# Modulation products of a two-layer mixer network: units of 256 columns behind every second block, in place of 128 columns behind each

## The chip, the cores and the metric

The kernel runs on one core of a Trainium2 chip. The metric is the device time of one execution in microseconds, the median of a few runs. Besides these runs, one execution was taken by the hardware profiler; everything said below of single instructions comes from that one.

## What is computed

The reference is a network of two layers over 512 latent and 256 context tokens of 1024 features. Each layer first turns the conditioning vector `c` (for the latent tokens) and `c_ctx` (for the context tokens) into six vectors of 1024 numbers, the modulation: shift, scale and gate of the first half of the layer, shift, scale and gate of the second.

```python
m_lat = jnp.split((silu_c @ ada_w[l] + ada_b[l])[:, None, :], 6, axis=-1)
m_ctx = jnp.split((silu_cc @ ada_w[l] + ada_b[l])[None, None, :], 6, axis=-1)
xn_lat = modulate(rmsnorm(h_lat, norm1_w[l]), m_lat[0], m_lat[1])
...
h_lat = h_lat + m_lat[2] * merge_branches(...)
h_lat = h_lat + m_lat[5] * conv_ffn(modulate(rmsnorm(h_lat, norm2_w[l]), m_lat[3], m_lat[4]), ...)
```

`ada_w[l]` is 1024 by 6144. The product has two rows only (one for each conditioning vector), but it reads all 25 MB of the matrix in each layer. The rest of a layer is an input projection, three mixers (an mLSTM, an attention with shared keys, a gated delta net), their merge and output projection, and a gated feed forward network with a short convolution.

## The kernel before, in words

**Large products.** `gemm_fm` (L227) makes a product feature-major, one block of 128 output columns at a time. For a block it loads raw weights (`wraw`, L208, one DMA from SyncE's queue into one of 3 slots of 4 KB in each partition, tag `wraw`), splits them into a high and a low float32r part (`wsplit`, L216: a copy on ScalarE, a subtraction on VectorE), multiplies (`mm3`, L241: three matmuls for each of 8 blocks of the contraction, high by high L248, high by low L249, low by high L250, first for the 512 latent tokens, then for the 256 context tokens where they count), and hands the PSUM banks to `done`, which evicts them.

**The modulation in between.** The first 16 of the 96 blocks of 128 modulation columns are made at the start of the kernel, 512 columns at a time (`ada_mm`, L428). The other 80 are made one by one in `ada_unit` (L457), called at three kinds of place: after each block of `gemm_fm` while the counter `self.nada` is above zero (L235 to L239), and four in a row in `ada_fill` (L473) three times, where the norm of the next part is being made. The counter is set to 32 in the mixers of layer 0, to 16 in the feed forward part of layer 0 and to 20 in the mixers of layer 1.

A unit works like this. Its raw weights, 8 blocks of 128 rows by 128 columns (512 KB), come through the same `wraw` slots. Then the transpose of the unit before is issued (`ada_fin`, L481). Then come 8 float32 matmuls (L467): the stationary operand is 32 columns wide, of which two count, and four blocks of the contraction lie side by side in the four column groups of the array. The profile shows two records for each of these matmuls, 16 for a unit. ScalarE copies the result out of PSUM (L470). In the next call of `ada_fin` the TensorE turns it (L489) and VectorE adds the four groups (L491); with every eighth block of columns the bias is added.

```python
def ada_unit(self):
    ...
    raw = self.wraw(self.I["ada_w"][l][:, 128 * g:128 * g + 128], KD, 128, f"ad{l}_{g}")
    self.ada_fin()
    ps = self.adps[0](f"adp{l}_{g}")
    for k in range(KD):
        j = k % 4
        nc.tensor.matmul(ps[32 * j:32 * j + 32, 0:128], self.s32[:, 2 * k:2 * k + 32], raw[:, k, :],
                         start=(k < 4), stop=(k >= 4), tile_position=(0, 32 * j))
    rw = self.T([128, 128], f"adr{l}_{g}", tag="adr")
    nc.scalar.copy(rw, ps[:, 0:128])
```

**PSUM.** The unit's product takes a bank of tag `pc` in the mixers and in the feed forward part. There is one such bank, and in the mixers of layer 0 it is also the one that the context tokens of the large products use. The transpose takes one of the two banks `pl` of the latent tokens in the mixers, and a bank `pa` in the feed forward part.

**What sets the order.** The program is traced in the order of `PLAN` (L43), and a scheduler that simulates the engines then puts the instructions of each engine in order: of those that are ready it takes the one with the highest priority. The scans of the delta net (`g0`, `g1`) and the attention (`ga`) have high priorities, the large products and the units fill the time in between. So a unit or a block of a product can be cut: small steps of a scan are put between its matmuls. SyncE's queue issues nearly all DMAs, strictly in its own order.

Of the kernel before, what the change touches and what calls it, by code (L numbers as in the profile page):

```python
# [16 lines left out]
D = 1024  # L17
# [12 lines left out]
# columns of the input projection  # L30
# [5 lines left out]
# token tiles 0..3 are latent, 4 and 5 context; scan orders of the two directions  # L36
ORDER = ((4, 5, 0, 1, 2, 3), (5, 4, 3, 2, 1, 0))

# The mixers of each layer: the order in which their parts are traced, the priorities of the parts and of the weights
# (the long chains of small steps first, the large products in between), the PSUM of the context tokens in P1.  # L40
# P0, P1: projections of the delta net's pairs of heads, g0, g1: their scans; qp, ga: attention; mp, ml: mLSTM;
# cz, ao, mg: gates; n: from here on columns of the modulation in between.
# [51 lines left out]
class Kernel:  # L94
# [7 lines left out]
    # ---------------------------------------------------------------- pools  # L102
# [18 lines left out]
    # slots of the mixers' phase: a.. for the delta net, b.. for the others, gs for the projections  # L121
# [21 lines left out]
    # slots of the phase of the merge and the feed forward  # L143
# [12 lines left out]
    # PSUM banks: latent and context tokens of the large products, the delta net, the others  # L156
# [3 lines left out]
    def p0(self):  # L160
        """Banks of the latent tokens: those of the context tokens too where there are none."""
        self.turn = not self.turn
        return self.pb if self.spare and self.turn else self.pl
# [14 lines left out]
    # ---------------------------------------------------------------- small helpers  # L178
    def rsqrt(self, out, z, n, nm, who="n"):
        """out = z ** -0.5 for [128, n] float32 z (bit trick and Newton steps)."""  # L180
# [19 lines left out]
    def split(self, h, l, x, eng=None):  # L200
        """x = h + l, both in float32r."""
# [5 lines left out]
    # ---------------------------------------------------------------- weights  # L207
    def wraw(self, src, nk, ncols, nm, slot=None):  # L208
        """raw weights [128, nk, ncols] from src rows (k p), columns given."""
        t = slot(nm) if slot else self.T([128, 1024], nm, tag="wraw", bufs=3)  # L210
# [16 lines left out]
    def gemm_fm(self, src, c0, ncols, nk, segs, done, nm):  # L227
        """Feature-major product: columns c0.. of src [nk*128, *] as stationary, tokens moving.
        segs: list of (token range, xh [128, nk, n], xl), latent first.
        done(block, [(psum, token range)]) takes the result."""  # L230
        for b in range(ncols // 128):
# [3 lines left out]
            if self.nada:  # L235
                self.nada -= 1
                self.ada_unit()
                if self.nada == 0:
                    self.ada_fin()  # L239
# [14 lines left out]
    def first_weights(self, src, c0, nk, nm, slot=None):  # L254
        """Weights for gemm_first."""
# [16 lines left out]
    def first_part(self, segs, nk, k0, k1, a, e):  # L272
        """Blocks k0.. of the contraction for the tokens a..."""
# [4 lines left out]
        for k in range(k0, k1):  # L278
            for b in range(2):
                ps = self.fp[s][b][:, sl]  # L280
                hw, lw = self.fw(k, b)
                # one accumulation group for the bank
# [4 lines left out]
    def gemm_first(self, nk, segs, done, nm, begun=False):  # L287
        """gemm_fm of two blocks, side by side, that can start with the first block of features."""
# [8 lines left out]
    def gemm_tail(self, src, segs, done, nm, slot, nxt=None):  # L297
        """Feature-major product over two blocks of the contraction, all of its D columns, by groups of 256 tokens;
        done(block, token range, psum)."""
# [18 lines left out]
    def gemm_tm(self, src, c0, ncols, xs, done, nm, nlat=0):  # L318
        """Token-major product in groups of 256 columns: done(group, [(pair of tiles, psum)]); the first nlat groups
        for the latent tokens only."""  # L320
        nc = self.nc
        for g in range(ncols // 256):
            pss = [(self.pl if i < 2 else self.pc)(f"{nm}p{g}_{i}") for i in range(2 if g < nlat else 3)]
            for half in range(2):
# [3 lines left out]
                for i, ps in enumerate(pss):  # L328
                    for u in range(2):
# [3 lines left out]
                        for kk in range(4):  # L333
                            k = 4 * half + kk
                            xh, xl = xs[s][1][:, k, o:o + 128], xs[s][2][:, k, o:o + 128]
                            # one accumulation group for the bank
# [5 lines left out]
    # ---------------------------------------------------------------- setup  # L342
# [360 lines left out]
    def gates(self, l, xs):  # L703
# [102 lines left out]
        def c4(d, tt):                                              # columns of (dir, tile) in 48s  # L806
            return slice(24 * d + 4 * tt, 24 * d + 4 * tt + 4)
# [1106 lines left out]
```

## Time and profile before

| | |
|---|---|
| median of 3 runs | 2726.53 us (2725.04 to 2727.49) |
| span of the profiled execution, first to last instruction | 2715.6 us |
| TensorE busy | 2663.0 us, 98% |
| TensorE weight loads busy | 2261.6 us, 83% |
| VectorE, ScalarE, GpSimd busy | 58%, 37%, 9% |
| mean granted TensorE clock | 0.994 |
| modulation matmuls (L467), busy | 65.5 us |

The profiler gives no whole-execution time beside the span; the median of the runs lies 10.9 us above the span. Below, PE is the TensorE's matmul stream, PEld its weight loads (which overlap it), DVE is VectorE, ACT ScalarE, POOL GpSimd, SP SyncE, and L with a number is a line of the kernel. A TensorE record lasts from the entry of its first column until its results are out, so records of successive matmuls overlap; the cost of a matmul in a stream is the distance from its start to the next start.

### The profile page before, as it was taken

Reading aid. Unit: us, or ns where it says so; the run is one execution under the profiler, and the core shown is the slowest. Engines: PE = TensorE matmul, PEld = TensorE weight load, DVE = VectorE, ACT = ScalarE, POOL = GpSimd, SP = SyncE. Lnnn points to the kernel's source line nnn. Section 1 sums busy time; section 2 is a strip of 40 time slices with the busy share of each in tenths; the row PEclk is TensorE's granted clock in tenths of the full one; section 3 lists DMA queues with packets and bytes.
Section 4 is the critical chain, followed back from the end, with each engine's and each line's share of the span. In section 5 each row is a group of like instructions: output and inputs, shape, how many; then the busy total and the mean of one; then the engine's idle time right before and its main releaser. Section 6 shows DMA issues by size and latency. Waiting matters only on the chain.

```text
span 2715.6 us, 46016 instructions
## 1 busy us (share of the span) xinstructions
PE 2663.0 (98%) x18041; PEld 2261.6 (83%) x18041; DVE 1573.4 (58%) x3527; ACT 998.5 (37%) x2269; POOL 235.0 (9%) x234
## 2 busy tenths in 40 slices
PE   7999999999999999999999999999999999999999
PEld 5887988788888888888888899888877777888887
DVE  6775665756524655444444577867675646655555
ACT  5433354333322234232232254444633332433332
POOL 1000000000000410010010120000000003100000
PEclk9999999999999999999999999999998999999999
DMA  8354332556746423412212254422376675333332
GB/s 281 96 162 127 90 113 80 155 149 172 210 145 223 140 88 104 140 47 74 66 47 78 61 152 121 138 61 79 114 215 179 169 237 156 114 95 95 93 97 86
DMA packets 523466, 342.97 MB, mean 126 GB/s; under 512 B 48007, under 2 KB 488561, under 8 KB 522481
## 3 DMA queue, kind: packets, MB, share of 16 engines
q1 hardware_dynamic: 522961, 336.88, 42.2%
q8 instruction: 142, 2.33, 0.3%
q10 hardware_dynamic: 288, 3.15, 0.3%
q14 instruction: 75, 0.61, 0.1%
HBM read 283.92 MB, written 56.03 MB: 125 GB/s over the span
## 4 chain that ended last, share of the span: by engine, by line
PE 88%; DMA 5%; DVE 3%; ACT 1%; issue 1%; SPq 1%; POOL 0%; DVEq 0%; ACTq 0%; POOLq 0%
PE mg04p L249 2%; PE mg04p L250 2%; PE adp L467 2%; PE mg04p L248 2%; PE y0p L248 1%; PE y0p L250 1%; PE y0p L249 1%; PE mg14p L248 1%; PE mg14p L250 1%; PE mg14p L249 1%; PE y1p L248 1%; PE y0op L248 1%; PE y0op L250 1%; PE y0op L249 1%; PE y1p L249 1%
## 5 line engine op out<-in xcount | busy, mean ns | idle before, releaser
L1714 POOL TENSOR_TENSOR f0a<-f0a,f0g 128x768 f32<-128x768 f32 x22 | 40.7, 1848 | 486.8 <-DVE f0a L1702 486.8
L467 PE MATMUL adp<-ad,s 128*32 128x128 f32 x1280 | 65.5, 283 | 2.7 <-DVE cz0t L903 2.4
L1714 POOL TENSOR_TENSOR f1a<-f1a,f1g 128x512 f32<-128x512 f32 x22 | 28.5, 1294 | 315.4 <-DVE f1a L1702 284.4
L467 PEld LDWEIGHTS adp<-ad,s 128*32 128x32 f32 x1280 | 33.9, 110 | 26.0 <-issue 9.9
L1716 DVE TENSOR_TENSOR f0gl<-f0a,f0gh 128x768 fp32r<-128x768 f32 x22 | 21.1, 959 | 58.4 <-ACT f0gh L1715 58.4
L1715 ACT CAST f0gh<-f0a 128x768 fp32r<-128x768 f32 x22 | 18.3, 832 | 76.6 <-POOL f0a L1714 76.6
L1638 POOL TENSOR_TENSOR y0a<-y0a,y0g 128x768 f32<-128x768 f32 x16 | 33.0, 2062 | 129.9 <-DVE y0g L1635 127.6
L470 ACT COPY adr<-adp 128x128 f32<-128x128 f32 x80 | 21.2, 265 | 39.7 <-PE adp L467 39.3
L901 ACT ACTIVATE mg0t<-mg04p 128x512 f32<-128x512 f32 (+1 forms) x40 | 19.4, 486 | 38.5 <-PE mg04p L250 28.2
L1708 ACT ACTIVATE f0g<-f0g 128x768 f32<-128x768 f32 x22 | 18.5, 845 | 33.2 <-DVE f0g L1702 33.2
L1638 POOL TENSOR_TENSOR y1a<-y1a,y1g 128x512 f32<-128x512 f32 x16 | 23.9, 1494 | 78.3 <-DVE y1g L1635 78.3
L491 DVE TENSOR_REDUCE ada<-adc 128x2 f32<-128x8 f32 x80 | 12.9, 161 | 27.9 <-PE adc L489 27.6
L1635 DVE SCALAR_TENSOR_TENSOR y0g<-y0g,y0p 128x512 f32<-128x512 f32 (+1 forms) x32 | 17.4, 549 | 15.7 <-PE y0p L250 14.7
L1708 ACT ACTIVATE f1g<-f1g 128x512 f32<-128x512 f32 x22 | 13.8, 631 | 32.9 <-DVE f1g L1702 32.9
L979 DVE SCALAR_TENSOR_TENSOR m0mb<-m0mb,g0a,cst 128x128 f32<-128x128 f32 x48 | 14.0, 346 | 18.4 <-DMA m0mb<-g0rd 18.4
L489 PE MATMUL adc<-cst,adr 128*128 128x128 f32 x80 | 22.2, 278 | 0.4 <-ACT adr L470 0.4
L1659 DVE SCALAR_TENSOR_TENSOR hr<-y0op,y0gh,hr 128x512 f32<-128x512 f32 (+1 forms) x16 | 9.8, 615 | 21.0 <-PE y0op L250 21.0
L1002 PE MATMUL m0n<-m0vb,m0mb 128*128 128x129 f32 x96 | 19.1, 299 | 1.1 <-issue 1.1
L1611 DVE TENSOR_TENSOR y0l<-y0ld,y0h 128x768 fp32r<-128x768 f32 x12 | 13.0, 1093 | 12.2 <-ACT y0h L1610 12.2
L1734 DVE SCALAR_TENSOR_TENSOR hr<-f0d8p,ada,hr 128x512 f32<-128x512 f32 (+1 forms) x16 | 9.9, 618 | 15.7 <-PE f0d8p L250 15.7
L1734 DVE SCALAR_TENSOR_TENSOR hr<-f0d12p,ada,hr 128x512 f32<-128x512 f32 (+1 forms) x16 | 9.9, 618 | 15.7 <-PE f0d12p L250 15.7
L1734 DVE SCALAR_TENSOR_TENSOR hr<-f0d4p,ada,hr 128x512 f32<-128x512 f32 (+1 forms) x16 | 9.9, 618 | 15.7 <-PE f0d4p L250 15.7
(3922 smaller groups left out, 9921.5 us busy)
## 6 DMA issues: line engine op xcount, KB each, us to landing
ad<-ada_w SPq DMA_DIRECT2D x96, 512.0 KB, 4.0
mg04r<-w_in SPq DMA_DIRECT2D x20, 512.0 KB, 5.2
mg14r<-w_in SPq DMA_DIRECT2D x20, 512.0 KB, 5.1
y0g<-mg SPq DMA_DIRECT2D x24, 384.0 KB, 4.2
mg<-mg0t SPq DMA_DIRECT2D x24, 256.0 KB, 2.0
y0r<-w_branch SPq DMA_DIRECT2D x12, 512.0 KB, 3.9
mg<-mg1t SPq DMA_DIRECT2D x24, 256.0 KB, 4.3
y1r<-w_branch SPq DMA_DIRECT2D x12, 512.0 KB, 4.2
```

The costliest lines, as they stand in the source:

```text
L248: nc.tensor.matmul(o, hv[:, k, :], xh[:, k, :], start=(k == 0), stop=False)
L249: nc.tensor.matmul(o, hv[:, k, :], xl[:, k, :], start=False, stop=False)
L250: nc.tensor.matmul(o, lv[:, k, :], xh[:, k, :], start=False, stop=(k == nk - 1))
L467: nc.tensor.matmul(ps[32 * j:32 * j + 32, 0:128], self.s32[:, 2 * k:2 * k + 32], raw[:, k, :], start=(k < 4), stop=(k >= 4), tile_position ...
L470: nc.scalar.copy(rw, ps[:, 0:128])
L489: nc.tensor.transpose(ps[:, 128:256], rw, self.ident)
L901: nc.scalar.activation(s, o, AF.Tanh, scale=0.5)
L1638: nc.gpsimd.tensor_tensor(out=a[:, :nt], in0=a[:, :nt], in1=gt[:, :nt], op=ALU.add)
L1708: nc.scalar.activation(a[:, :nt], a[:, :nt], AF.Silu)
L1714: nc.gpsimd.tensor_tensor(out=a[:, :nt], in0=a[:, :nt], in1=keep[b][:, :nt], op=ALU.mult)
L1716: nc.vector.tensor_tensor(out=gl[:, k, :nt], in0=a[:, :nt], in1=gh[:, k, :nt].bitcast(F32), op=ALU.subtract)
L1734: nc.vector.scalar_tensor_tensor(out=hv[:, a:b], in0=ps, scalar=self.ada[l][:, 40 + j, (a >= SEQ):(a >= SEQ) + 1], in1=hv[:, a:b], op0=ALU ...
```

## The change

Units of 256 columns take the place of units of 128: 40 units where there were 80. Each loads its weights with two DMAs of 4 blocks by 256 columns (512 KB each, in two `wraw` slots), issues 8 matmuls of 256 columns and one copy of 256 columns; `ada_fin` turns it with two transposes and reduces it with one instruction. A new function `ada_next` takes the place of the lines in `gemm_fm`: it counts the blocks as before, but calls `ada_unit` at every second one only, the first among them. `ada_fill` is called for 2 units instead of 4. The raw weights have 4 slots instead of 3 (also where the gates' weights are loaded, L674), and the scratch for dynamic DMA is set to 1024. The other lines of the diff remove comments.

```diff
 def wraw(self, src, nk, ncols, nm, slot=None):
-        t = slot(nm) if slot else self.T([128, 1024], nm, tag="wraw", bufs=3)
+        t = slot(nm) if slot else self.T([128, 1024], nm, tag="wraw", bufs=4)
...
 def gemm_fm(self, src, c0, ncols, nk, segs, done, nm):
...
             done(b, self.mm3(hv, lv, nk, segs, f"{nm}p{b}"))
-            if self.nada:
-                self.nada -= 1
-                self.ada_unit()
-                if self.nada == 0:
-                    self.ada_fin()
+            self.ada_next()
...
 def ada_unit(self):
-        raw = self.wraw(self.I["ada_w"][l][:, 128 * g:128 * g + 128], KD, 128, f"ad{l}_{g}")
+        W = self.I["ada_w"][l]
+        raws = [self.wraw(W[512 * q:512 * q + 512, 256 * g:256 * g + 256], 4, 256, f"ad{l}_{g}_{q}") for q in range(2)]
         self.ada_fin()
         ps = self.adps[0](f"adp{l}_{g}")
-        for k in range(KD):
-            j = k % 4
-            nc.tensor.matmul(ps[32 * j:32 * j + 32, 0:128], self.s32[:, 2 * k:2 * k + 32], raw[:, k, :],
-                             start=(k < 4), stop=(k >= 4), tile_position=(0, 32 * j))
-        rw = self.T([128, 128], f"adr{l}_{g}", tag="adr")
-        nc.scalar.copy(rw, ps[:, 0:128])
+        for q, raw in enumerate(raws):
+            for j in range(4):
+                k = 4 * q + j
+                nc.tensor.matmul(ps[32 * j:32 * j + 32, 0:256], self.s32[:, 2 * k:2 * k + 32], raw[:, j, :],
+                                 start=(q == 0), stop=(q == 1), tile_position=(0, 32 * j))
+        rw = self.T([128, 256], f"adr{l}_{g}", tag="adr")
+        nc.scalar.copy(rw, ps[:, 0:256])
...
+def ada_next(self):
+        if self.nada:
+            self.nada -= 1
+            if self.nada % 2:
+                self.ada_unit()
+            if self.nada == 0:
+                self.ada_fin()
...
 def ada_fin(self):
-        nc.tensor.transpose(ps[:, 128:256], rw, self.ident)
-        a = self.ada[l][:, g:g + 1, :]
-        nc.vector.tensor_reduce(out=a, in_=ps[:, 128:256].rearrange("p (o j r) -> p o r j", o=1, j=4)[:, :, 0:2, :],
+        for b in range(2):
+            nc.tensor.transpose(ps[:, 256 + 128 * b:384 + 128 * b], rw[:, 128 * b:128 * b + 128], self.ident)
+        nc.vector.tensor_reduce(out=self.ada[l][:, 2 * g:2 * g + 2, :],
+                                in_=ps[:, 256:512].rearrange("p (o j r) -> p o r j", o=2, j=4)[:, :, 0:2, :],
                                 axis=AX.X, op=ALU.add)
...
-                    self.ada_fill(4)
+                    self.ada_fill(2)
...
-    nc = bacc.Bacc("TRN2", target_bir_lowering=False, num_devices=1)
+    nc = bacc.Bacc("TRN2", target_bir_lowering=False, num_devices=1,
+                   dynamic_dma_scratch_size=1024)
```

## Rows read from the trace of the kernel before

**Rows 1.** The page: span, busy time of each engine, clock in 40 slices.
```profile
span 2715.6 us, 46016 instructions
...
PE 2663.0 (98%) x18041; PEld 2261.6 (83%) x18041; DVE 1573.4 (58%) x3527; ACT 998.5 (37%) x2269; POOL 235.0 (9%) x234
...
PEclk9999999999999999999999999999998999999999
```

**Rows 2.** The page: share of the chain that ended last, by engine.
```profile
PE 88%; DMA 5%; DVE 3%; ACT 1%; issue 1%; SPq 1%; POOL 0%; DVEq 0%; ACTq 0%; POOLq 0%
```

**Rows 3.** The page's costliest groups: busy us, mean ns of one, idle before, releaser.
```profile
L467 PE MATMUL adp<-ad,s 128*32 128x128 f32 x1280 | 65.5, 283 | 2.7 <-DVE cz0t L903 2.4
...
L470 ACT COPY adr<-adp 128x128 f32<-128x128 f32 x80 | 21.2, 265 | 39.7 <-PE adp L467 39.3
...
L489 PE MATMUL adc<-cst,adr 128*128 128x128 f32 x80 | 22.2, 278 | 0.4 <-ACT adr L470 0.4
```

**Rows 4.** Timeline of PE around one unit, feed forward, layer 0: start, duration, instructions.
```profile
1057.71 0.28 PE L250 MATMUL f0g02p<-n01xh,f0g02s0l 128*128 128x256 f32 x1
1057.83 0.27 PE L489 MATMUL adc<-cst,adr 128*128 128x128 f32 x1
1058.03 0.64 PE L467 MATMUL adp<-ad,s 128*32 128x128 f32 x16
1058.61 0.49 PE L248 MATMUL f0g02p<-n01xh,f0g02s1h 128*128 128x512 f32 x1
```

**Rows 5.** Groups of PE's lines: the records of the 512-column units, columns as in rows 3.
```profile
L438 PE MATMUL ad<-ad,s 128*32 128x512 f32 x64 | 10.1, 599 | 2.0 <-issue 1.2 <-DMA ad<-ada_w 0.8
```

**Rows 6.** Timeline of PE at the start: two units of 512 columns, three transposes.
```profile
41.09 3.64 PE L438 MATMUL ad<-ad,s 128*32 128x512 f32 x32
44.66 0.55 PE L449 MATMUL adc<-cst,adr 128*128 128x128 f32 x3
```

**Rows 7.** Timeline of PE: the first unit that is cut, and the last piece of all.
```profile
228.54 0.40 PE L250 MATMUL aq0p<-n00xh,aq0s1l 128*128 128x512 f32 x1
228.86 0.64 PE L467 MATMUL adp<-ad,s 128*32 128x128 f32 x14
229.43 0.24 PE L1545 MATMUL c00z<-c00XT,c00N 32*32 32x32 f32 x2
229.60 0.41 PE L467 MATMUL adp<-ad,s 128*32 128x128 f32 x2
229.94 0.43 PE L1220 MATMUL b0a4po<-b0a4P,b0v 128*64 128x128 f32 x2
...
2339.18 0.41 PE L467 MATMUL adp<-ad,s 128*32 128x128 f32 x2
```

**Rows 8.** Waits of PE: who waited for whom, us in total, times, longest.
```profile
PE adp L467 <- DVE cz0t L903: 2.4, 1, 2.4
...
PE g1ps L691 <- DVE g1w L205: 1.1, 1, 1.1
...
PE mg14p L248 <- ACT mg1t L901: 1.1, 1, 1.1
...
PE g0ps L691 <- DVE g0w L205: 1.0, 1, 1.0
...
PE bp0p L337 <- ACT bp0s_0h L204: 0.8, 1, 0.8
...
PE mg04p L248 <- ACT mg0t L901: 0.7, 1, 0.7
```

**Rows 9.** Waits of SyncE's queue: the longest in total.
```profile
SPq L213 <- PE adp L467: 238.4, 57, 26.3
```

**Rows 10.** DMA issues: the modulation's weights, KB each, median us to landing.
```profile
ad<-ada_w SPq DMA_DIRECT2D x96, 512.0 KB, 4.0
```

**Rows 11.** Windows: busy time, then granted clock, DMA share, GB/s.
```profile
1005.00:1155.00 150.00, 147.70 (x1133) 125.90 (x1132) 79.47 (x158) 52.46 (x100) 9.63 (x8) 1.00 0.41 120
...
2062.00:2076.00 14.00, 13.79 (x76) 10.08 (x78) 4.82 (x20) 4.04 (x9) 0.00 (x0) 0.52 0.39 115
```

More of the change, by code (lines that the diff above doesn't have):

```diff
@@ L488, in ada_fin @@
         ps = self.adps[1](f"adc{l}_{g}")
-        nc.tensor.transpose(ps[:, 128:256], rw, self.ident)
-        a = self.ada[l][:, g:g + 1, :]
-        nc.vector.tensor_reduce(out=a, in_=ps[:, 128:256].rearrange("p (o j r) -> p o r j", o=1, j=4)[:, :, 0:2, :],
+        for b in range(2):
+            nc.tensor.transpose(ps[:, 256 + 128 * b:384 + 128 * b], rw[:, 128 * b:128 * b + 128], self.ident)
+        nc.vector.tensor_reduce(out=self.ada[l][:, 2 * g:2 * g + 2, :],
+                                in_=ps[:, 256:512].rearrange("p (o j r) -> p o r j", o=2, j=4)[:, :, 0:2, :],
                                 axis=AX.X, op=ALU.add)
-        if g % 8 == 7:
-            a = self.ada[l][:, g - 7:g + 1, :]
-            bb = self.vcol("ab", 48 * l + g - 7, 8)
+        if g % 4 == 3:
+            a = self.ada[l][:, 2 * g - 6:2 * g + 2, :]
+            bb = self.vcol("ab", 48 * l + 2 * g - 6, 8)
             nc.vector.tensor_tensor(out=a, in0=a, in1=bb.rearrange("p (b o) -> p b o", o=1).broadcast_to([128, 8, 2]),
@@ L673, in gates_mm @@
             nk = min(3, KD - k0)
-            raw = self.T([128, 1024], f"{nm}raw{k0}", tag="wraw", bufs=3)[:, :nk * n].rearrange("p (k c) -> p k c", k=nk)
+            raw = self.T([128, 1024], f"{nm}raw{k0}", tag="wraw", bufs=4)[:, :nk * n].rearrange("p (k c) -> p k c", k=nk)
             rows = W[128 * k0:128 * (k0 + nk), :].rearrange("(k p) c -> p k c", p=128)
@@ L1766, in start @@
         self.load_x()
-        self.adaq = [(l, g) for l in range(DEPTH) for g in range(48)][16:]
+        self.adaq = [(l, g) for l in range(DEPTH) for g in range(24)][8:]
         xs = self.N["xs"]
@@ L1825, in body @@
                 if l + 1 < DEPTH:
-                    self.ada_fill(4)
+                    self.ada_fill(2)
                     self.nada, self.adps = 16, (self.pc, self.pa)
                 else:
-                    self.ada_fill(4)
+                    self.ada_fill(2)
                 self.spare = nt < NT
```

## The prediction

> **What bounds the kernel now.** I read the busy times first: TensorE is busy for 2663.0 of 2715.6 us, so at most 52.6 us of the span can be won by waiting less; all else must come from fewer or shorter TensorE instructions [rows 1]. The chain of work that ended last says the same: 88% of it is TensorE [rows 2]. The granted clock is full in almost every slice [rows 1]. VectorE at 58% and ScalarE at 37% are not the limit. Next come the costliest groups: the modulation's matmuls L467 are the largest of TensorE's groups with 65.5 us, with a transpose (L489) for each of 80 units [rows 3]. Last I read TensorE's timeline around single units, since a record's duration (0.27 us) is mostly latency and the distances between starts are the cost.
>
> The sum is made against the profiled execution (span 2715.6 us). The median of the runs is 10.9 us above it; I carry that unchanged and subtract from 2726.5.
>
> **The change, part by part.**
>
> *Visits.* A unit that is not cut, in the feed forward part [rows 4]: the last product matmul starts at 1057.71, the next product at 1058.61, 0.90 us later, where the ordinary step of that product is 0.12 (1057.71 to 1057.83). A unit with its transpose costs 0.78 us of TensorE. The 16 records take 0.64: four rounds of four column groups, and one record's 0.27 at the end, so a round takes (0.64 - 0.27) / 3 = 0.12. For 256 columns the trace has no row; the bounds are this one and the 512-column units of the start, 32 records in 3.64 us, eight rounds, with 0.60 for one record [rows 5, 6], so a round takes (3.64 - 0.60) / 7 = 0.43. The step from 128 to 512 columns is even, so I take a third of it: a round of 256 columns takes 0.12 + 0.31 / 3 = 0.22, its last record 0.27 + 0.33 / 3 = 0.38. The 16 records then span 3 x 0.22 + 0.38 = 1.04 instead of 0.64, 0.40 more. The second transpose behind the first costs (0.55 - 0.27) / 2 = 0.14 as an upper value [rows 6]; back to back with a warm array I take 0.12. The new visit costs 0.78 + 0.40 + 0.12 = 1.30, two old ones 1.56: 0.26 saved for a pair. Reading errors of 0.02 in four rows make it 0.20 to 0.30; I take 0.24. Times 40 pairs: **9.6 us less**, 8 to 12. What is saved is the entry and exit of a visit, not streaming: four old and two new rounds stream the same columns.
>
> A rule bears on the size of this. The Trainium skill, TensorE: Matmul & The Clock Gate, Measured speedup vs the span model, gives a pack of tiles one matmul's duration and some 4 ns for each further tile. Were four such packs to follow one another, an old unit would be 4 x 0.28 = 1.1 us and a new one 4 x 0.39 = 1.6, and 40 pairs would save 26 us. The trace differs: 16 records fit into 0.64 us [rows 4], so successive packs overlap, and the measurement decides.
>
> *Cuts.* 20 of the 80 units are cut by small steps into 56 pieces, 36 cuts; the first is 14 records and 2 records, the last piece lies at 2339.18 [rows 7]. Price: the piece of 14 occupies 228.54 to 229.43 less an ordinary step of 0.23, 0.66, as much as a whole unit; the piece of 2 adds 0.34 to its successor and some 0.1 at its entry, so a cut costs 0.4. Checked by the group: 65.5 us busy less 80 x 0.64 = 51.2 leaves 14.3 for 36 cuts, 0.4 each [rows 3, 4]. After the change a lone piece has two rounds that are 0.10 longer each, so a cut costs 0.6. Their number is the unknown. Counted by places between matmuls (80 x 7 before, 40 x 7 after) it would be 18, counted by the time that units take about 30, and a unit that lies open longer could meet more. I take 28, nearer to the count by time since a scan step becomes ready by the clock: 28 x 0.6 = 16.8 against 14.3, **2.5 us more**, between 3.5 less and 15 more.
>
> *Waits for banks.* TensorE waits 2.4 us for the context bank before the first unit, and 1.1 and 0.7 us before large products whose bank rotates with the transpose of a unit: 4.2 in all [rows 8]. With half the visits half of it should go, but the first and longest wait is before a unit that stays where it is. **1.5 us less**, between 4.2 less and 3 more, since a bank is held longer by 0.5 us in each visit.
>
> *The fourth slot.* Three waits for split weights, 1.1, 1.0 and 0.8 us, lie where raw weights came late [rows 8], and SyncE's queue waited 238.4 us in 57 issues for a unit's matmuls to free a slot [rows 9]. Order of the slots before: block, unit, block, unit over three, so the load of block b + 2 waits for the matmuls of unit b and everything behind it in SyncE's order waits too. After: block, unit, unit, block over four; a block's load waits only for a split, two blocks earlier. The loads are as many and as large (80 of 512 KB, 4.0 us to landing [rows 10]). The splits themselves stay. **1.5 us less**, between nothing and 2.9.
>
> *Free.* 80 copies of 0.265 us become 40 longer ones on ScalarE [rows 3], the reductions on VectorE go from 80 to 40, and the scratch setting has no operation in the trace that waits for it; all lie beside TensorE work. If that cover were gone, ScalarE's 80 copies are worth at most 21.2 us in all and the saving is less than half of it.
>
> Sum: -9.6 + 2.5 - 1.5 - 1.5 = -10.1. Forecast 2716.4 us, 0.37% faster.
>
> **Rivals.**
>
> *Given back (2724).* TensorE's work shrinks but the span doesn't follow, because scans and norms set the ends. For it: in the mixers units only fill holes, and the 12 units of the three fills lie in the shadow of a norm. Against it: TensorE has few holes at all [rows 1], and in the stretch with the 16 feed forward units it is busy for 147.70 of 150 us [rows 11]. There 8 pairs would still give 8 x 0.24 = 1.9; with a little elsewhere the time is 2724, no change that can be measured.
>
> *Cut more (2736).* The scheduler fits the longer units worse and cuts them more. Each cut costs 0.6, so the gain of the visits is gone at (14.3 + 9.6) / 0.6 = 40 cuts, and the kernel is 0.2% (5.5 us) slower from 49 on. At 55 cuts it is 33.0 - 14.3 - 9.6 = 9 us slower, 2736. For it: a unit in the mixers is open for 1.3 us instead of 0.8, beside scans that have priority. Against it: there are half as many. The Trainium skill, TensorEngine Tiling (Array Packing), Key Properties, says that a change of the tiling mode drains the engine; by that rule each cut pays. The trace agrees: the piece of two records costs 0.4 us [rows 7].
>
> *A slow stretch goes (2709).* From 2062 to 2076 the granted clock is 0.52, the lower of the two levels, behind small matmuls and a wait; those 14 us hold 7 us of work at full clock [rows 11]. The units lie in that part of layer 1. If the new order keeps the engine busier before it, 7 us more are won: 2709. As well a new such stretch could come elsewhere; I hold a shift of this kind possible in either direction, and the gain a little less likely than not.
>
> That the change doesn't do what it says is hardly possible: the counts of units follow from the counter and the fills (16 + 8 + 10 + 6 = 40).
>
> **How the numbers follow.** Forecast 0.56, slow stretch gone 0.10, given back 0.21, cut more 0.13. Differences within 0.2% (5.5 us) can hardly be told from no change, so faster takes the first two, 0.66, no change 0.21, slower 0.13. The forecast's own bounds, with all terms at their good or bad ends half the time, are about 2706 to 2725. The range 2702 to 2728 holds these, the given-back case and most of the case of the slow stretch, and leaves out the cut case (0.13) and the rest.
>
> **What would show it.** Right: L467 with 640 records and a busy time of about 40 x 1.04 + 0.6 x cuts, near 58 us instead of 65.5; a visit in the feed forward part of 1.3 us against 0.90 + 0.66; pieces fewer than 70; TensorE's busy time down by about 8 us, its idle time by 3. Wrong: rounds of more than 0.22 us; more than 40 cuts; a TensorE busy time that falls by 8 us while the idle time grows as much; a second stretch at the lower clock.

## The result, and the profile after

The changed kernel takes 2709.14 us (median of 4 runs, 2707.44 to 2711.38) against 2725.78 us for the kernel before beside it (2722.26 to 2727.49): ratio 0.9944, 95% interval 0.9930 to 0.9958. Two later measurements of the same kernel gave 0.9967 (0.9955 to 0.9979) and 0.9954 (0.9940 to 0.9968). By these ratios it is 0.3 to 0.6% faster, 9 to 15 us; the forecast was 10.1 us. (The ratios on record are not the plain quotients of the medians: the medians of the three measurements lie 16.6, 10.4 and 15.6 us below those of the kernel before beside them.) The forecast time was 2716.4 us; the first measurement lies 7.3 us below it, inside the range.

The page after: span, busy times, clock, the chain that ended last, and the groups of the units' matmuls and copies (columns as in [rows 1 to 3]).

```profile
span 2706.8 us, 44597 instructions
...
PE 2648.6 (98%) x17401; PEld 2245.3 (83%) x17401; DVE 1569.9 (58%) x3487; ACT 995.6 (37%) x2229; POOL 238.5 (9%) x234
...
PEclk9999999999999999999999999999999999999999
...
PE 87%; DVE 5%; DMA 4%; issue 1%; SPq 1%; ACT 1%; POOL 0%; DVEq 0%; ACTq 0%; POOLq 0%
...
L465 PE MATMUL adp<-ad,s 128*32 128x256 f32 x640 | 53.1, 396 | 0.0
...
L468 ACT COPY adr<-adp 128x256 f32<-128x256 f32 x40 | 14.9, 373 | 25.6 <-PE adp L465 24.7
```

The span is 8.8 us shorter than that of [rows 1]. TensorE's busy time fell by 14.4 us (2663.0 to 2648.6), so what is left of the span, its idle time, rose from 52.6 to 58.2 us: some 40% of what TensorE saves is waited away again. The units' busy time fell from 65.5 to 53.1 us.

Where that went is read from the four windows between these landmarks: the start, the first product of the feed forward part of layer 0, the first product of the scan in layer 1, the first product of the feed forward part of layer 1, the end. Columns: window and its length; busy time and instructions of each engine; granted clock; DMA share; GB/s. First the kernel before, then the changed one.

```profile
0.00:1008.40 1008.40, 976.41 (x7354) 837.55 (x7354) 587.02 (x1511) 381.34 (x1008) 87.31 (x99) 0.99 0.50 149
1008.40:1588.90 580.50, 578.11 (x3628) 503.90 (x3628) 290.82 (x473) 179.39 (x288) 54.37 (x36) 1.00 0.27 81
1588.90:2331.70 742.80, 729.01 (x5273) 608.98 (x5273) 489.41 (x1255) 305.30 (x780) 64.11 (x76) 0.99 0.51 147
2331.70:2715.60 383.90, 379.50 (x1788) 311.18 (x1788) 206.15 (x291) 132.48 (x196) 29.19 (x23) 0.99 0.32 95
```

```profile
0.00:1002.90 1002.90, 971.58 (x7098) 831.26 (x7098) 581.32 (x1495) 377.95 (x992) 89.46 (x99) 0.99 0.49 150
1002.90:1581.80 578.90, 576.21 (x3468) 501.05 (x3468) 290.03 (x463) 179.24 (x278) 54.35 (x36) 1.00 0.27 82
1581.80:2325.60 743.80, 724.60 (x5080) 605.07 (x5080) 492.54 (x1243) 305.65 (x768) 65.49 (x76) 0.99 0.50 147
2325.60:2706.80 381.20, 376.16 (x1756) 307.96 (x1756) 205.98 (x289) 132.79 (x194) 29.18 (x23) 1.00 0.32 94
```

Layer 0 up to its feed forward part gains 5.5 us, that feed forward part 1.6, the last part 2.7. The mixers of layer 1 gain nothing: TensorE is busy for 4.4 us less there and the stage is 1.0 us longer (in later profiles 745.9 us twice for the changed kernel, 745.2 for the kernel before with the scratch setting of the change). The last part's 2.7 us are the clock's: in the kernel before it begins with 6.8 us at 1.2 GHz (granted clock 0.50), which are busy throughout and so cost some 3.4 us. Where the kernel before, with the scratch setting of the change, had the full clock there, this part took 380.9 us, no more than the 381.2 here.

```profile
2332.20:2339.00 6.80, 6.80 (x53) 5.63 (x51) 5.50 (x16) 3.03 (x7) 0.71 (x1) 0.50 0.27 80
```

One visit in the feed forward part, as in [rows 4] (timeline of PE: start, duration, instructions):

```profile
1052.73 0.28 PE L246 MATMUL f0g02p<-n01xh,f0g02s0l 128*128 128x256 f32 x1
1052.85 0.38 PE L497 MATMUL adc<-cst,adr 128*128 128x128 f32 x2
1053.16 1.07 PE L465 MATMUL adp<-ad,s 128*32 128x256 f32 x16
1054.16 0.50 PE L244 MATMUL f0g02p<-n01xh,f0g02s1h 128*128 128x512 f32 x1
```

From 1052.73 to 1054.16 is 1.43 us; less the ordinary step of 0.12 the visit costs 1.31, where two old ones cost 1.56: 0.25 less for a pair. A round of four column groups takes (1.07 - 0.38) / 3 = 0.23.

And a unit that is cut, in the mixers of layer 0 (same columns), as in [rows 7]:

```profile
273.39 1.06 PE L465 MATMUL adp<-ad,s 128*32 128x256 f32 x14
274.39 1.16 PE L1419 MATMUL c00wp<-c00S,c00kq 128*128 128x128 f32 x8
275.48 0.62 PE L465 MATMUL adp<-ad,s 128*32 128x256 f32 x2
276.03 0.50 PE L244 MATMUL ak0p<-n00xh,ak0s1h 128*128 128x512 f32 x1
```

The 14 records occupy 1.00 us, as long as all 16 above (1053.16 to 1054.16); the piece of two adds 0.55. Followed through the whole timeline, the 40 units lie in 57 pieces, 17 cuts, where the 80 units had 36.

Last, waits (who waited for whom, us in total, times, longest): the gate product's in the kernel before, then PE's in the changed kernel, the copy of ScalarE that ended the longest of them (timeline, with the idle time before it in brackets), and SyncE's queue:

```profile
PE mg10p L248 <- ACT mg1t L901: 2.1, 1, 2.1
```

```profile
PE mg10p L244 <- ACT mg1t L909: 6.0, 1, 6.0
...
PE cz00p L244 <- DVE ada L498: 2.1, 1, 2.1
PE m1pu L955 <- DVE ada L498: 2.1, 1, 2.1
...
PE g0ps L699 <- DVE g0w L205: 1.0, 1, 1.0
PE g1ps L699 <- DVE g1w L205: 1.0, 1, 1.0
PE bp0p L333 <- ACT bp0s_0h L204: 0.8, 1, 0.8
```

```profile
2197.17 0.60 ACT L909 ACTIVATE mg1t<-mg10p 128x512 f32<-128x512 f32 x1 [6.19 <-DMA c1y<-c11on]
```

```profile
SPq L213 <- PE adp L465: 180.4, 35, 32.3
```

The wait of the first unit for the context bank (2.4 us in [rows 8]) is gone. Two of 2.1 us stand where a large product (cz00p) and the mLSTM (m1pu) wait for the reduction of a unit, which now reads two transposes from the bank that they want. The gate product mg10p waits 6.0 us, before 2.1: the copy that empties its bank sits behind 6.19 us in which ScalarE is idle until the delta net's last result is written (c1y<-c11on). The three waits for weights of [rows 8] are all but unchanged: 1.0, 1.0 and 0.8 against 1.1, 1.0 and 0.8.

### The profile page after: what moved, and what is told of

Read it like the earlier page. It is cut to its first block, busy times and chain, and to the rows that moved or that the text cites. A ratio compares the mean times of both kernels' runs of the same rounds, so it can differ in the third digit from the quotient of the medians.

```text
span 2706.8 us, 44597 instructions
## 1 busy us (share of the span) xinstructions
PE 2648.6 (98%) x17401; PEld 2245.3 (83%) x17401; DVE 1569.9 (58%) x3487; ACT 995.6 (37%) x2229; POOL 238.5 (9%) x234
## 4 chain that ended last, share of the span: by engine, by line
PE 87%; DVE 5%; DMA 4%; issue 1%; SPq 1%; ACT 1%; POOL 0%; DVEq 0%; ACTq 0%; POOLq 0%
PE mg04p L244 2%; PE mg04p L246 2%; PE mg04p L245 2%; PE adp L465 2%; PE y0p L244 1%; PE y0p L245 1%; PE y0p L246 1%; PE mg14p L244 1%; PE mg14p L246 1%; PE mg14p L245 1%; PE y1p L244 1%; PE y1p L245 1%; PE y1p L246 1%; PE y0op L244 1%; PE y0op L246 1%
## 5 line engine op out<-in xcount | busy, mean ns | idle before, releaser
L465 PE MATMUL adp<-ad,s 128*32 128x256 f32 x640 | 53.1, 396 | 0.0
L465 PEld LDWEIGHTS adp<-ad,s 128*32 128x32 f32 x640 | 18.2, 110 | 18.4 <-issue 6.7
L909 ACT ACTIVATE mg0t<-mg04p 128x512 f32<-128x512 f32 (+1 forms) x40 | 19.4, 486 | 25.3 <-PE mg04p L246 23.7
L1716 ACT ACTIVATE f1g<-f1g 128x512 f32<-128x512 f32 x22 | 13.8, 632 | 33.0 <-DVE f1g L1710 33.0
L468 ACT COPY adr<-adp 128x256 f32<-128x256 f32 x40 | 14.9, 373 | 25.6 <-PE adp L465 24.7
L1742 DVE SCALAR_TENSOR_TENSOR hr<-f0d0p,ada,hr 128x512 f32<-128x512 f32 (+1 forms) x16 | 9.9, 617 | 21.0 <-PE f0d0p L246 21.0
L1619 DVE TENSOR_TENSOR y0l<-y0ld,y0h 128x768 fp32r<-128x768 f32 x12 | 12.9, 1093 | 13.8 <-ACT y0h L1618 13.8
L989 ACT ACTIVATE m0mb<-m0mb 128x512 f32<-128x512 f32 x12 | 7.6, 631 | 31.1 <-DVE m0mb L987 22.8
```

Source lines behind the costliest of these rows:

```text
L465: nc.tensor.matmul(ps[32 * j:32 * j + 32, 0:256], self.s32[:, 2 * k:2 * k + 32], raw[:, j, :], start=(q == 0), stop=(q == 1), tile_positio ...
L909: nc.scalar.activation(s, o, AF.Tanh, scale=0.5)
L1716: nc.scalar.activation(a[:, :nt], a[:, :nt], AF.Silu)
L1742: nc.vector.scalar_tensor_tensor(out=hv[:, a:b], in0=ps, scalar=self.ada[l][:, 40 + j, (a >= SEQ):(a >= SEQ) + 1], in1=hv[:, a:b], op0=ALU ...
```

## The experiments

Theory A: the gain is the entry and exit of 40 visits that are no longer made (0.24 us each). Its rivals are the other things the change touches: the scratch setting, the slots, the places of the units, the form of the loads, the cuts. (Beside the lines shown and the comments, a few lines of the change fit the list of units and the index of the bias to the new width; they alter no work.)

### The scratch setting, the slots, the units: one at a time

The kernel before with the scratch of 1024:

```diff
-    nc = bacc.Bacc("TRN2", target_bir_lowering=False, num_devices=1)
+    nc = bacc.Bacc("TRN2", target_bir_lowering=False, num_devices=1,
+                   dynamic_dma_scratch_size=1024)
```

> The kernel before with the scratch for dynamic DMA at 1024 and nothing else. If the gain of 16.6 us is all the units' (theory A), the time is that of before within 0.2% and the span too. The span of the profiled execution fell by 8.8 us only, so a rival (theory B) puts the other 8 us outside the span and down to the scratch: then this kernel is about 8 us faster than before, with the same span.

Measured: 2720.72 us, ratio 0.9997 (0.9984 to 1.0010), span 2716.6. The setting does nothing that can be measured.

The same with the fourth slot for raw weights, and the units of 128 columns as they were:

```diff
-        t = slot(nm) if slot else self.T([128, 1024], nm, tag="wraw", bufs=3)
+        t = slot(nm) if slot else self.T([128, 1024], nm, tag="wraw", bufs=4)
```

> The kernel before with the scratch at 1024 and four slots for raw weights, units of 128 columns behind every block as before. Theory A: the slot alone is worth 0 to 3 us, the forecast's 1.5. A rival (theory C) makes the slot the cause of the gain, since the queue of SyncE is blocked for less time: 10 us or more faster than before, and SyncE's wait for the units' matmuls well under 238 us.

Measured: 2727.30 us, ratio 1.0018 (1.0005 to 1.0032), span 2721.5. Alone the slot gives nothing, and rather costs 5 us; SyncE's queue waits longer for the units' matmuls, 258.4 us in 57 issues.

The changed kernel with three slots, and the old scratch:

```diff
-        t = slot(nm) if slot else self.T([128, 1024], nm, tag="wraw", bufs=4)
+        t = slot(nm) if slot else self.T([128, 1024], nm, tag="wraw", bufs=3)
...
-    nc = bacc.Bacc("TRN2", target_bir_lowering=False, num_devices=1,
-                   dynamic_dma_scratch_size=1024)
+    nc = bacc.Bacc("TRN2", target_bir_lowering=False, num_devices=1)
```

> Units of 256 columns behind every second block, with three slots and the scratch as before. Theory A: about 10 to 15 us faster than before, TensorE busy some 14 us less as in the changed kernel. Theory B: 8 us less of a gain than the changed kernel. Theory C: no faster than before, since two loads of a unit now share three slots with the blocks.

Measured: 2714.20 us, ratio 0.9972 (0.9959 to 0.9986), PE busy for 2653.1 us.

And with three slots and the scratch of 1024:

> The changed kernel with three slots instead of four. Against the run with three slots and the old scratch it tells what the scratch does (theory A: nothing; theory B: 8 us less), against the changed kernel what the slot does (theory A: 0 to 3 us; theory C: 10 us or more).

Measured: 2713.39 us, ratio 0.9971 (0.9957 to 0.9985), PE busy for 2651.9 us. The wide units alone carry half of the gain or more: 0.28% of 0.33 to 0.56%. With three slots the scheduler also cuts them more often, 21 times instead of 17. What the fourth slot adds to them is the distance from 0.9971 to the three measurements of the changed kernel, 0.9967, 0.9954 and 0.9944: 0.04 to 0.27%, in different measurements, with intervals that overlap or nearly touch. Whether it helps the wide units stays open.

### The changed kernel again

> The changed kernel once more, on one chip with the next three. Theory A (fewer entries and exits of a visit, fewer cuts): 0.4 to 0.7% faster than before. With three slots the units alone gave 0.29%; what it has beyond that is the slot's share.

Measured: 2710.58 us, ratio 0.9967 (0.9955 to 0.9979), span 2709.2. Its feed forward part of layer 0 has the full clock throughout (1.00) and takes 577.7 us:

```profile
1004.60:1582.30 577.70, 574.71 (x3468) 500.28 (x3468) 289.71 (x463) 179.10 (x278) 54.32 (x36) 1.00 0.27 82
```

That is 2.8 us below the 580.5 of the kernel before, for ten pairs of visits: 0.28 a pair, against 0.24 forecast. The changed kernel's first profile showed only 1.6 there because its stage begins with 3.4 us at 1.2 GHz, which cost up to half of that:

```profile
1003.80:1007.20 3.40, 3.40 (x24) 2.11 (x24) 3.40 (x11) 2.12 (x6) 0.71 (x1) 0.51 0.22 62
```

The other profiles agree. With half of each stretch at 1.2 GHz taken off, this stage takes 579.5 to 580.5 us in the kernel before, the two runs with narrow units above and the run with halved units below, and 577.2 to 577.9 us in the three profiles of the changed kernel and the two runs with three slots. Neither the kernel before nor the changed kernel has a cut unit in this stage, so the difference there is that of the visits.

### The place: two narrow units in a row

The kernel before with four slots, the scratch of 1024, and two units of 128 columns behind every second block. In the program's order, places and loads per place are those of the change, and the number of units is the old one.

```diff
-                self.ada_unit()
+                if self.nada % 2:
+                    self.ada_unit()
+                    self.ada_unit()
```

> Units of 128 columns as before, but two in a row behind every second block, with four slots and the scratch of the change: the place of the change without its width. Theory A: nothing gained, within 0.3% of before, TensorE busy within 3 us of before, since each of the 80 units still pays its entry, exit and transpose. A rival (theory P, the place): the gain comes from disturbing the products half as often, then most of the 0.5% is here too.

Measured: 2742.65 us, ratio 1.0091 (1.0075 to 1.0107). PE's waits:

```profile
PE adp L469 <- DVE cz0t L905: 8.8, 2, 6.8
...
PE adc L491 <- ACT adr L472: 4.3, 10, 0.6
PE adp L469 <- ACT mg0t L903: 4.2, 3, 1.7
```

The order that ran is not the one that was meant. Ten of the 40 pairs stand directly one behind the other; between the units of the other 30 the scheduler put other work, so most units kept a place of their own (in the feed forward part of layer 0 all of them, where a visit with its transpose takes 0.89 to 1.01 us from product to product at the full clock, against 0.90 before). In the ten, the second unit begins with the transpose of the first, which waits for ScalarE's copy (ten times, 4.3 us), and units wait for the one bank they share with the context tokens (8.8 us). TensorE is idle for 80.7 us (span 2750.0, busy 2669.3). So narrow units traced in pairs are no substitute for wide ones. Whether fewer places would be a gain in themselves, with narrow units that do follow each other, this run doesn't test.

### Further along the same road: units of 512 columns

Twenty units of 512 columns behind every fourth block, four loads of 512 KB for each, a whole bank, four transposes.

```diff
-        raws = [self.wraw(W[512 * q:512 * q + 512, 256 * g:256 * g + 256], 4, 256, f"ad{l}_{g}_{q}") for q in range(2)]
+        raws = [self.wraw(W[256 * q:256 * q + 256, 512 * g:512 * g + 512], 2, 512, f"ad{l}_{g}_{q}") for q in range(4)]
...
-            if self.nada % 2:
+            if self.nada % 4 == 3:
```

> The change taken one step further: 20 units of 512 columns behind every fourth block, four loads each. Theory A: a visit costs 227 ns less for each two units merged, 0.24 x 20 = 4.8 us of TensorE less than the changed kernel, and if cuts come by places between matmuls (6 in 100 of them in both kernels) there are 9 for 17, so TensorE is busy 5 to 8 us less. If cuts come by the time that a unit lies open, there are as many as in the changed kernel or more and cost 1 us each. Theory D (given back where a scan ends): TensorE's busy time falls so, the time does not.

Measured: 2739.14 us, ratio 1.0071 (1.0058 to 1.0085). A unit in the feed forward part of layer 0 (timeline of PE, with the load of the next block's weights by SyncE's queue; in brackets the idle time before, and its releaser):

```profile
1088.85 0.28 PE L246 MATMUL f0a02p<-n01xh,f0a02s0l 128*128 128x256 f32 x1
1089.06 1.92 PE L466 MATMUL adp<-ad,s 128*32 128x512 f32 x16
1090.15 0.37 SPq L213 DMA_DIRECT2D f0a02r<-w_up  x1
1091.72 0.65 PE L498 MATMUL adc<-cst,adr 128*128 128x128 f32 x4 [0.73 <-ACT adr L469]
1095.17 0.80 PE L244 MATMUL f0a02p<-n01xh,f0a02s1h 128*128 128x512 f32 x1 [2.80 <-ACT f0a02s1h L204]
1095.76 0.63 PE L245 MATMUL f0a02p<-n01xl,f0a02s1h 128*128 128x512 f32 x1
```

The unit's own matmuls behave: a single record takes 0.59, so a round takes (1.92 - 0.59) / 3 = 0.44. But its four loads take all four slots, so the next block's weights come late: their load (f0a02r) is issued at 1090.15, when the unit's matmuls are under way, and after the unit TensorE waits 0.73 for its copy and 2.80 for a split. Then the clock is down too (granted 0.50 from 1094.30 to 1101.10); the products that follow take 0.80 and 0.63, where such a record takes 0.40 at the full clock [rows 7]. The stage takes 595.3 us instead of 578.9, and TensorE is idle for 81.7 us in all (span 2738.5, busy 2656.8). Another 14.3 us are lost before that stage (1017.2 us against 1002.9), with one wait of 5.7 us of a unit for the context bank. The 20 units are cut 11 times, near the 9 of the count by places. So with these slots the road ends at 256 columns. That more slots would open it again is not shown: no such run was made.

### The cuts

The changed kernel with the units' matmuls at the highest priority, so that nothing is put between them.

```diff
-                nc.tensor.matmul(ps[32 * j:32 * j + 32, 0:256], self.s32[:, 2 * k:2 * k + 32], raw[:, j, :],
-                                 start=(q == 0), stop=(q == 1), tile_position=(0, 32 * j))
+                with self.high(10 ** 6):
+                    nc.tensor.matmul(ps[32 * j:32 * j + 32, 0:256], self.s32[:, 2 * k:2 * k + 32], raw[:, j, :],
+                                     start=(q == 0), stop=(q == 1), tile_position=(0, 32 * j))
```

> The changed kernel with the units' matmuls at the highest priority of all, so that nothing is put between them. Theory A with the cuts as a true cost: 40 pieces instead of 57, TensorE busy about 12 us less, and the time by up to 12 us. Theory D: the busy time falls, but TensorE's idle time grows as much, since the steps of the scans that were put between the matmuls now come later.

Measured: 2714.66 us, ratio 0.9976 (0.9965 to 0.9987). The page's PE and the units' group:

```profile
PE 2648.8 (98%) x17401; PEld 2247.8 (83%) x17401; DVE 1567.7 (58%) x3487; ACT 994.4 (37%) x2229; POOL 237.7 (9%) x234
...
L466 PE MATMUL adp<-ad,s 128*32 128x256 f32 x640 | 45.8, 404 | 0.0
```

Two cuts are left of 17 and the units' busy time falls by 7.3 us, but TensorE is busy as long as in the changed kernel (2648.8 against 2648.6) and the kernel is no faster (its median is 4.1 us above the 2710.58 of the changed kernel on the same chip, with intervals that overlap). The rest of TensorE's work took 7.5 us more. A part of it is the clock (0.991 on the mean against 0.993: 0.002 of 2700 us, some 5 us of longer records), the remainder is not isolated: a small step that doesn't cut a unit still has to run between other matmuls. A cut's price shows in the units' rows; avoiding it in this way is not won.

### The form of the loads

The changed kernel's loads (rows of 1 KB, 40 units), but half of a unit's columns behind each of two blocks: 80 visits again, and six slots since the weights stay for two visits.

```diff
+    def ada_half(self, i):
...
+        c = slice(128 * i, 128 * i + 128)
...
-                nc.tensor.matmul(ps[32 * j:32 * j + 32, 0:256], self.s32[:, 2 * k:2 * k + 32], raw[:, j, :],
+                nc.tensor.matmul(ps[32 * j:32 * j + 32, 0:128], self.s32[:, 2 * k:2 * k + 32], raw[:, j, c],
...
             if self.nada % 2:
                 self.ada_unit()
+            else:
+                self.ada_half(1)
```

> The changed kernel's loads (40 units of 256 columns, rows of 1 KB) but the old number of visits: the first 128 columns are multiplied behind one block, the other 128 behind the next, with a transpose in each visit. Six slots for raw weights, since a unit's weights stay for two visits. Theory A (the gain is the entry and exit of 40 visits, 0.24 us each): it is lost. 2 x 0.78 us of visits in place of 1.31 for a pair, so some 9 us above the changed kernel beside it, ratio to the kernel before 0.998 to 1.002, TensorE busy for 2660 us or more. Theory L (the gain comes from fewer and larger loads of the weights): it stays, ratio 0.994 to 0.997, as the changed kernel beside it.

Measured: 2726.28 us, ratio 1.0011 (0.9998 to 1.0024), beside 0.9954 for the changed kernel on the same chip. Its stages, as above:

```profile
0.00:1023.00 1023.00, 981.13 (x7353) 842.42 (x7353) 583.69 (x1496) 382.58 (x1009) 88.52 (x99) 0.98 0.49 149
1023.00:1603.00 580.00, 577.99 (x3628) 504.19 (x3628) 288.78 (x462) 179.64 (x287) 54.31 (x36) 1.00 0.27 80
```

Two visits in the feed forward part (timeline of PE), the one with the second half of a unit and the next with the first half of another:

```profile
1062.32 0.28 PE L246 MATMUL f0a00p<-n01xh,f0a00s1l 128*128 128x256 f32 x1
...
1063.11 0.50 PE L244 MATMUL f0g02p<-n01xh,f0g02s0h 128*128 128x512 f32 x1
...
1071.57 0.28 PE L246 MATMUL f0g02p<-n01xh,f0g02s0l 128*128 128x256 f32 x1
...
1072.58 0.50 PE L244 MATMUL f0g02p<-n01xh,f0g02s1h 128*128 128x512 f32 x1
```

The two transposes of a unit stand together in every second visit, not one in each as was expected, but the pair costs what was expected: 0.79 and 1.01 us less 0.12 each, 1.56, against 1.31 for a wide visit.

The gain is gone with the loads left as they were, and TensorE is busy for 2664.2 us, as before. So the loads alone are not its source. The clean stage is the feed forward part, at the full clock: 580.0 us, 2.3 above the 577.7 with wide units, 0.23 a pair. The layer 0 mixers before it lose more than visits can explain (14.6 us on the kernel before): 4.2 us before a unit's bank, 4.0 us before a gate whose weights come late, and a clock of 0.98. In all this kernel is 19.4 us slower than the changed kernel on the same chip (2726.28 and 2706.85), where theory A had some 9. The part beyond that is not theory A's; it may be the six slots' and the order's, which was not taken apart.

### Does the scan set the time in the mixers of layer 1?

The changed kernel without the ten units that its blocks of layer 1 would run (their columns are set to a constant by one memset).

```diff
-                self.nada = 20 if l else 32
+                self.nada = 0 if l else 32
```

> The changed kernel without the 10 units that run in the mixers of layer 1 (their 2560 modulation columns are left out and hold a constant instead). From the start of the scan's products of layer 1 to the first gate product of its feed forward part the changed kernel took 743.8 us, the kernel before 742.8. Theory A (TensorE's work sets the time in this stage): 10 x 1.31 us and the cuts go, so the stage shrinks by 12 to 16 us, to 728 to 732. Theory D (the end of the delta-net's scan sets the time there, and what units save is given back in the wait for its last exchange): the stage shrinks by less than 5 us, to 739 or more, and the wait of the gate product before that point grows beyond its 6.0 us.

Measured: 2683.41 us, ratio 0.9863 (0.9847 to 0.9878). The mixers of layer 1, and the wait before the gate product:

```profile
1580.70:2296.70 716.00, 703.25 (x4901) 597.09 (x4901) 490.09 (x1230) 301.83 (x758) 64.52 (x76) 0.99 0.48 138
```

```profile
PE mg10p L244 <- ACT mg1t L910: 3.1, 1, 3.1
```

The stage shrinks by 27.8 us (743.8 to 716.0), and the wait becomes shorter, not longer. Theory D falls: the end of the scan does not alone set the time of this stage, since units taken out whole shorten it. That every microsecond saved there comes through is not shown; the 4.4 us that the change itself saved did not. Theory A's 12 to 16 us were too few. TensorE's busy time shrinks by 21.4 us, its idle time by 6.4. The busy time is near what visits and cuts cost: the stage had ten cuts, which go with the ten units, so 10 x 1.31 + 10 x 0.6 = 19.1 us, and its stretches at 1.2 GHz fall from 17.0 to 10.2 us, up to 3.4 us more. The expectation had too few cuts and no idle time. The 27.8 us are those of one pair of profiles; the medians of the two kernels on this chip (2706.85 and 2683.41) are 23.4 us apart, 2.3 a unit.

### The new waits for a reduction

The changed kernel with a unit's product and the transposes of the unit before in the two halves of one bank.

```diff
-        self.ada_fin()
         ps = self.adps[0](f"adp{l}_{g}")
+        self.ada_fin(ps)
...
-        ps = self.adps[1](f"adc{l}_{g}")
+        if ps is None:
+            ps = self.adps[0](f"adc{l}_{g}")
```

> The changed kernel with the product of a unit and the transposes of the unit before it in the two halves of one bank, so that no bank of the large products or of the context pool is taken for a transpose. Theory W (the new waits of large products for the reduction of a unit, 2.1 + 2.1 us, are on the path): 2 to 4 us below the changed kernel beside it, idle time of TensorE down by as much. Theory N (such waits only stand where another wait would): within 1.5 us of the changed kernel beside it; or slower by up to 4, since the transposes now wait for the same bank as the product.

Measured: 2706.23 us, ratio 0.9950 (0.9933 to 0.9966), beside the unaltered changed kernel on the same chip:

> The changed kernel unaltered, beside the three others on the same chip. From its two earlier measurements, 0.9944 and 0.9967 of the kernel before, I expect 0.994 to 0.997, and TensorE busy for 2649 to 2651 us.

Measured: 2706.85 us, ratio 0.9954 (0.9940 to 0.9968). The waits that are left of the kind, in the kernel with one bank:

```profile
PE mg10p L244 <- ACT mg1t L910: 1.6, 1, 1.6
...
PE adp L465 <- DVE ada L499: 0.6, 1, 0.6
```

Both waits of 2.1 us are gone, the one of 6.0 has become 1.6, and the time is the same. So is TensorE's idle time: 58.0 us (span 2714.3, busy 2656.3), against 58.8 in the changed kernel (2709.3, 2650.5). Theory N holds: taking these waits away shortens nothing; what stands in their place was not followed up. No version here that does the whole work is measurably faster than the changed kernel.

## Why the prediction was right, and where its steps were wrong

The direction, the mechanism and the range were right. That the span's 8.8 us came so near the forecast's 10.1 is in part luck: TensorE's busy time fell by 14.4 us, twice the 7.1 that the terms of visits and cuts add up to (the prediction says about 8), and its idle time grew by 5.6 us where it was to fall by 3. The steps:

- **Visits** (9.6 us less): right. A visit costs 1.31 us (forecast 1.30), a round 0.23 (0.22). The two transposes of a visit delay the unit by 0.31 us (1052.85 to 1053.16) where one delays it by 0.20 [rows 4]: the second adds 0.11 (0.12). At the full clock the feed forward part gives 0.28 a pair with the change and loses 0.23 again when the visits are halved but the loads are not. By the rule of the Trainium skill, TensorE: Matmul & The Clock Gate, Measured speedup vs the span model, the unit's product alone would take 1.6 us if its four packs followed one another, an estimate; the trace does not agree, the product takes 1.07. (The 26 us that the prediction works out by that rule are 24 by its rounded figures, 40 x (2 x 1.1 - 1.6), and 27 unrounded; nothing else rests on them.)
- **Cuts** (2.5 us more): wrong in sign. "I take 28, nearer to the count by time": there are 17, what the count by places gave (18). Their price was right: the lone piece of two takes 0.55 us instead of 0.34. By the group, 53.1 less 40 x 1.07 = 42.8 leaves 10.3 us for 17 cuts, 0.6 each. So this term was 4.0 us less in the units' rows. Visits (40 x 0.25 = 10.0) and cuts together are 14.0 of the 14.4 us that TensorE's busy time fell. But the step was also incomplete: with 15 cuts avoided by priority nothing was won, so a cut's price cannot be added to the time as if nobody else would pay it. Whether the cuts that the change saved reached the time is not shown by itself.
- **Waits for banks** (1.5 us less): wrong. The first wait did not stay, it went; two others of 2.1 us came, and TensorE's idle time grew by 5.6 us, nearly all of it in the mixers of layer 1 (13.8 to 19.2 us). The prediction counted waits that it saw and halved them. In the new waits a bank is still being read by the reduction of a unit, now of two transposes, and the kernel with one bank shows that taking these waits away brings nothing either: their sum is no term.
- **The fourth slot** (1.5 us less): its evidence was wrong. The three waits for weights that it was to shorten are all but unchanged after. SyncE's queue did wait less, 180.4 us in 35 issues against 238.4 in 57 [rows 9], but that is the wide units': with three slots and wide units it waited 152.6 us in 39 issues, with four slots and narrow units 258.4 in 57. The slot alone gained nothing; what it gives to the wide units stays open.
- **Free**: right for the time. ScalarE's copies fell to 14.9 us, and TensorE waits 0.5 us for one of them in all; the scratch setting shows nothing. The reductions on VectorE are fewer, but the two waits of 2.1 us are for them, so that part was not free in the trace, though it cost no time.
- **Given back** was partly true, in one stage. In the mixers of layer 1 TensorE's busy time fell by 4.4 us and the stage did not shrink. Idle time took its place, most visibly before mg10p. The reason given, that scans set the ends, is half right: that wait does end with the delta net's last result (6.19 us of ScalarE's idle time, 0.63 in the kernel before), but without units the stage is 27.8 us shorter, so the scan does not hold its end alone, and the kernel with one bank has 1.6 us in place of this wait and is no faster. The wait moves with the order of the instructions; why the order of the changed kernel has it is not isolated.
- **A slow stretch goes**: the one from 2062 went and others came. The stretches at 1.2 GHz add up to 37 us before and 39 after, so the clock gives nothing over the whole span; it moves gains between stages (the last part gained by it, the first feed forward part lost).
- **The 10.9 us around the span**: wrong. The run that left the after profile took 2708.54 us for a span of 2706.8, 1.8 us more, and the profiled execution of the kernel before with the new scratch 2718.39 for 2716.6, again 1.8. The span of 2715.6 came from a quick execution: in the later measurements the kernel before ran between 2711 and 2732 us. So the sum was made against a quick execution and subtracted from an ordinary one, without harm here since only the difference was used; but a single pair of spans has an uncertainty of several microseconds, as large as each smaller term.

The three smaller terms were to sum up to 0.5 us less. In their place the cuts gave 4.0 us and the idle time took 5.6, so the span fell by about the forecast although of the four terms only the first was right. The time itself fell by 10.4 to 16.6 us between medians; what lies beyond the span's 8.8 is within what executions of one kernel differ by, and no run here assigns it to a cause.

## What to carry to other kernels

Where an extra job visits a busy engine, price the visit: entry, exit, and the latency of its last result. Halving the number of visits at equal streamed columns gains just that where TensorE sets the time (here the feed forward part), and the trace gives it to 0.05 us from the distances between starts; elsewhere idle time can take it back, as in the mixers of layer 1. Waits that are scattered over a scheduled kernel were no sum of terms here: two were removed and a third shortened, and the idle time stayed, so a forecast does better to leave them at nothing with a range of both signs. When a unit is widened, count the slots that its loads leave for the work around it: with all four taken, the gain was lost. And look whether the order that ran is the order that was meant before a run is read as a test.

## What was not expected of the hardware

Rounds of four column groups scale evenly: 0.12 us for 128 columns, 0.23 for 256, 0.44 for 512, with a fixed part of some 0.01 us only; the fixed part that a wider unit saves is that of the visit. Work between dense products is worth more than its own matmul records: ten units with 16.3 us of busy matmuls (18.42 with them, 2.14 without, by the windows of their tile alone) were worth 27.8 us of the stage in the mixers of layer 1. The rest can be named: 18 transposes, 2.8 us as an estimate from 0.31 a visit; up to 3.4 us of the clock (17 us of stretches at 1.2 GHz with the units, 10 without); and 6.4 us of idle time. And in the kernel with units of 512 columns the clock was at the lower level behind a unit, 0.73 us of waiting, four transposes and 2.80 us of waiting (0.50 from 1094.30 to 1101.10), in the midst of dense products.

```profile
1581.80:1960.70 378.90, 5.11 (x64) 1.70 (x64) 1.49 (x4) 1.00 0.37 107
1960.70:2178.30 217.60, 13.32 (x128) 3.99 (x128) 2.98 (x8) 0.98 0.67 190
```

```profile
1580.70:1955.40 374.70, 2.14 (x32) 0.83 (x32) 0.75 (x2) 1.00 0.37 105
```

These are the windows of the units' tile alone, in the mixers of layer 1 of the changed kernel and then of the one without their ten units (columns: length; PE, PEld and ACT busy; clock; DMA; GB/s): four units cost 5.11 us of records, eight cost 13.32, since the second stretch holds the scan's small steps and eight of the ten cuts.
